# Sixteen-wide inverse blocks, with their join issued in the running chain, in a kernel that interleaves RWKV-7 and sparse attention

## The chip, the cores and the metric

The kernel runs on one core of a Trainium2 chip. The metric is the device time of one execution in microseconds (us), as the median of three runs. TensorE, VectorE (DVE in the rows), ScalarE (ACT), GpSimd (POOL) and SyncE (SP, which issues most loads and stores) each work through a queue of their own in a fixed order.

## The reference

One step of a layer on 1,056 tokens: 1,024 of a prompt and 32 of a running stream (the "sample"). The normalised input is projected once; half of the columns feed sparse attention (8 query heads, 4 key heads, each query keeps its top k keys by a lightweight index), the other half feed RWKV-7 time mixing (8 heads of 64). Both results are joined, projected, and followed by an MLP with 4,096 hidden units. What matters here is RWKV's recurrence over tokens, per head with a 64 x 64 state:

```python
def step(S, inp):
    r_t, w_t, k_t, v_t, kk_t, b_t = inp
    s_kk = jnp.einsum('bhvk,bhk->bhv', S, kk_t)
    S = S * w_t[:, :, None, :] - s_kk[..., None] * b_t[:, :, None, :] + v_t[..., None] * k_t[:, :, None, :]
    return S, jnp.einsum('bhvk,bhk->bhv', S, r_t)
s_fin, y = lax.scan(step, wkv0, ...)
```

The kernel computes it by chunks of 64 tokens. Within a chunk the dependence of a token on the ones before is a triangular 64 x 64 system per head, and the chunk needs the inverse of that matrix.

## The kernel before

A first phase projects the input and finds the top k keys (`topk`, and the masks made of it). The last phase is the output projection and the MLP. Between them, from about 450 to 930 us of the profile, two generators are advanced in turn, one step each: `attn_all` (36 items: 4 key heads times 9 token tiles, each with scores, softmax, transposes and products) and `rwkv_all`. The program is written in that interleaved order; a scheduler then fixes the order of every engine's queue from the program order, the dependences and ranks, with its own estimate of durations. `tc.high_priority(n)` moves instructions n places ahead in rank, a negative n behind. All of `rwkv_all` stands under OFF (-200), a unit's chain additionally under BOFF (+300) and a unit's preparation under FOFF (-100).

RWKV works on five units: units 0 to 3 are 256 prompt tokens each, in four chunks, and unit 4 is the sample in one chunk. Round i of `rwkv_all` runs three generators side by side:

- `rwkv_front` of unit i+2 loads the unit's rows, makes the decays and keys, and for each chunk the matrix G of all eight heads (matmuls of line 712, mask on VectorE in line 715). The G buffer is the one of unit i, so chunk c waits until unit i has done its chunk c. At the end `lane_inverse` inverts the 32 x 32 diagonal blocks.
- `rwkv_back` of unit i is the chain: it first calls `rwkv_join`, which makes 64 x 64 inverses out of the 32 x 32 blocks with two rounds of 32 small TensorE calls (lines 768 and 776; every such call stands as two instructions in the trace). Then, chunk by chunk, pR, copy to `rh` (line 882), pU, copies to VU, pS, new state `st`, pY, copy to `y` on ScalarE (line 911). All four accumulators take the same single PSUM buffer `pc`.
- `rwkv_norm` of unit i-1 normalises and gates the result and stores it.

`lane_inverse` lays a unit's 32 x 32 blocks out with one pair of heads and chunks per partition: four VectorE transposes with every input column taken twice (line 824, 32 x 1,024 each), then 31 steps of two element-wise instructions on GpSimd (lines 829 and 831) on up to 136 elements per partition, and four transposes back into G (line 835), and for the full units two more into `X1` (line 840). The start value is loaded by DMA from `half`.

After both generators, `project_early` multiplies the first three token tiles by the output weights (line 1256), whose split into high and low parts waits until unit 3 is done.

Of the kernel before, what the change touches and what calls it, by code (L numbers as in the profile page):

```python
# [32 lines left out]
def pack(I):  # L33
    A={n:np.ascontiguousarray(I[n]) for n in RAW}
    A['pvec']=pvec(I)
    A['norms']=np.ascontiguousarray(np.concatenate([I['norm_mix'],I['norm_ffn']]))
    A['gains']=np.ascontiguousarray(np.stack([I['q_gain'][0],I['k_gain'][0],I['kidx_ln_g'][0],I['kidx_ln_b'][0]]))
    A['rope']=rope(); A['ident']=np.eye(128,dtype=np.float32); A['gmask']=gmask()
    p=np.arange(128)
    A['bones']=(p[:,None]//64==np.arange(2)[None]).astype(np.float32)  # L40
    A['bone2']=(p[:,None]//64==p[None]//64).astype(np.float32)
    s,m=np.arange(32)[None,:,None],np.arange(16)[None,None]
    A['half']=(s==2*m+(p[:,None,None]%32)//16).astype(np.float32).reshape(128,512)
    return A


# [7 lines left out]
F32 = mybir.dt.float32  # L54
# [509 lines left out]
def rwkv_setup(S):  # L564
    nc, I = S.nc, S.I
    S.gm = S.rs.tile([128, 128], F32, name="gm")
    nc.sync.dma_start(S.gm, I["gmask"])
    S.bones = S.rs.tile([128, 2], F32, name="bones")
    nc.sync.dma_start(S.bones, I["bones"])
    bone2 = S.rs.tile([128, 128], F32, name="tmp", bufs=2)  # L570
    nc.sync.dma_start(bone2, I["bone2"])
    S.cen = S.rs.tile([128, 128], F32, name="cen")
    nc.vector.scalar_tensor_tensor(S.cen, bone2, -1.0 / 64, S.ident, op0=ALU.mult, op1=ALU.add)
    S.ones = S.rs.tile([128, 64], F32, name="ones")
    nc.gpsimd.memset(S.ones, 1.0)
    S.hv = S.rs.tile([128, 4, 4], F32, name="hv")
    nc.gpsimd.tensor_scalar(S.hv[:, 0], S.pv[:, 56:60], 0.5, None, op0=ALU.mult)
    nc.gpsimd.tensor_scalar(S.hv[:, 1], S.pv[:, 56:60], -0.5, 1.0, op0=ALU.mult, op1=ALU.add)
    nc.gpsimd.tensor_scalar(S.hv[:, 2:4].rearrange("p a b -> p (a b)"), S.pv[:, 44:52], 0.5, None, op0=ALU.mult)
    S.g2 = S.rs.tile([96, 512], F32, name="g2")  # L580
    nc.sync.dma_start(S.g2, I["g2"][0])

    w = S.rs.tile([32, 2, 512], F32, name="tmp", bufs=2)
    nc.sync.dma_start(w[:, 0], I["w2"][0])
    nc.sync.dma_start(w[:, 1], I["a2"][0])
    S.w3 = S.rs.tile([96, 2, 512], F32R, name="w3")
# [9 lines left out]
def rwkv_front(S, u, U, B):  # L596
# [3 lines left out]
    w = n // NC  # L600
# [116 lines left out]

    while B and B.done < B.NC:
        yield
    lane_inverse(S, U, nc.vector if u in DINV else nc.gpsimd)  # L720
    S.fronts += 1
    yield

# [33 lines left out]
def rwkv_join(S, ps, U):  # L757

    nc = S.nc
    X1 = U.X1.rearrange("p (c h) t -> p c h t", c=4)  # L760

    def pc():
        return ps.tile([128, 512], F32, name="pc", bufs=1).rearrange("p (a b c) -> p a b c", a=4, b=4)
    p = pc()
    for cc in range(4):
        for hp in range(4):
            for par, b in ((0, 64), (1, 0)):
                nc.tensor.matmul(p[b + 32:b + 64, cc, hp], U.G[b:b + 32, par, cc, hp, 32:64], X1[b:b + 32, cc, hp],
                                 start=True, stop=True)
    for par, b in ((0, 64), (1, 0)):  # L770
        nc.scalar.copy(X1[b + 32:b + 64], p[b + 32:b + 64])
    p = pc()
    for cc in range(4):
        for hp in range(4):
            for par, b in ((0, 64), (1, 0)):
# [34 lines left out]
def lane_inverse(S, U, eng):  # L810


    nc = S.nc
    L = S.rf2.tile([128, 32, 32], F32, name="L", bufs=1)
    Y = S.rf2.tile([128, 32, 32], F32, name="Yl", bufs=1)[:, :, 0:16]
    tm = S.rf2.tile([128, 144], F32, name="tl", bufs=1)
    G = U.G
    nc.sync.dma_start(Y, S.I["half"].rearrange("p (s m) -> p s m", s=32))

    def part(par, p, b):  # L820
        return G[p:p + 32, par, :, :, 32 * b:32 * b + 32].rearrange("p c h t -> p (c h) t")
    groups = [(0, 64, 0), (0, 96, 1), (1, 0, 0), (1, 32, 1)]
    for g in groups:
        nc.vector.transpose(L[g[1]:g[1] + 32].rearrange("p s t -> p t s"),  # L824
                            part(*g).rearrange("p l t -> p t l")[:, :, None, :].to_broadcast([32, 32, 2, 16]))
    for j in range(31, 0, -1):
        m, w = j // 2, 16 - j // 2
        t_ = tm[:, 0:j * w].rearrange("p (a b) -> p a b", a=j)
        eng.tensor_tensor(t_, L[:, 0:j, j:j + 1].to_broadcast([128, j, w]),  # L829
                          Y[:, j:j + 1, m:16].to_broadcast([128, j, w]), op=ALU.mult)  # L830
        eng.tensor_tensor(Y[:, 0:j, m:16], Y[:, 0:j, m:16], t_, op=ALU.add)  # L831

    for g in groups:
        if g[2] == 0 or U.w == 64:
            nc.vector.transpose(part(*g).rearrange("p l (m d) -> p m d l", d=2), Y[g[1]:g[1] + 32].rearrange("p s m -> p m s"))
    if U.w == 64:
        U.X1 = S.P[0].tile([128, 16, 32], F32, name="X1", bufs=1)
        for par, p, b in groups:
            if b == 0:
                nc.vector.transpose(U.X1[p:p + 32], part(par, p, b))  # L840


def rwkv_back(S, rp, ps, U, state):
# [8 lines left out]
    def quarter(p):  # L852
        return p[:, 0:256].rearrange("p (a b) -> p a b", a=4)
    for c in range(len(U.tok), min(NC, 2)):
        U.tok.append(rwkv_tokens(S, rp, ps, U, c))
    tok = U.tok
    if w == 64:
        rwkv_join(S, ps, U)
    yield
    st = state.get("st")  # L860
    if u == 4:
# [7 lines left out]
    for c in range(NC):  # L869
# [31 lines left out]
            nc.vector.tensor_tensor(sn, pS, st, op=ALU.add)  # L901
            nc.vector.tensor_tensor(sn, sn, pcb, op=ALU.mult)
        yield
        pY = quarter(pc())
        for hp, par in pairs:
            nc.tensor.matmul(pY[PAR[par], hp], VU[:, par, hp], G[:, par, c, hp, 64:128], start=(hp == 0), stop=(first and hp == 3))
        if not first:
# [3 lines left out]
        nc.scalar.copy(y[:, :, c], pY)  # L911
        st = sn
        U.done = c + 1
        if c + 2 < NC:
            tok.append(rwkv_tokens(S, rp, ps, U, c + 2))
        elif U.next and TOKN and len(U.next.tok) < U.next.NC:
            U.next.tok.append(rwkv_tokens(S, rp, ps, U.next, len(U.next.tok)))
# [54 lines left out]


YB = 2


def rwkv_all(S, order):
# [23 lines left out]
    def norm(i):  # L1001
        if i >= 0:
            yield from rwkv_norm(S, S.P[0], S.ps, units[i])
        if 0 <= i + 2 < len(order):
            rwkv_prelude(S, S.P[0], units[i + 2])
    for i in range(-2, len(order) + 1):
        gens = []
        B = front = None
# [2 lines left out]
            gens.append(back := rwkv_back(S, S.P[0], S.ps, B, state))  # L1011
        if i >= -1:
            gens.append(norm(i - 1))
            if i == 0:
                shift_rows(S, S.P[0], S.ps)
        if i + 2 < len(order):
# [361 lines left out]
ATT0 = 0  # L1378
BOFF = 300
TOKB = 3  # L1380
FOFF = -100
EARLY = 0
POOLU0 = ('k','tha','KB0')
POOLU = ('tha',)
# [20 lines left out]
CKT = 6  # L1405
LAGT = 3
KNB = 5
OFF = -200


def body(tc, I, O, dbg=None):
# [126 lines left out]
```

## Time and profile before

| | us |
|---|---|
| median of 3 runs (lowest, highest) | 1,794.74 (1,794.37, 1,796.54) |
| the profiled execution | 1,798.12 |
| its span, first to last instruction | 1,796.3 |
| TensorE busy in the span | 1,663.9 (93%) |
| mean granted TensorE clock | 0.927 of full speed |

The busy time of an engine is the union of its instructions' times. The granted clock is 1 at 2.4 GHz and 0.5 at 1.2 GHz; a value in between is the mean over a stretch that holds both.

### The profile page before, as it was taken

The page shows a single profiled execution, that of the slowest core. Times are in us where ns is not written, and L with a number is a line of the kernel's source. Part 1 is how long each engine was busy: PE and PEld are TensorE (multiplying, and loading weights), DVE is VectorE, ACT ScalarE, POOL GpSimd, SP SyncE. Part 2 cuts the span into 40 slices and gives each one's busy share as a digit, 9 for nine tenths or more (in the row PEclk, how much of TensorE's full clock was granted, in tenths as well). Part 3 has the DMA queues.
Part 4 walks back from the last instruction along what each step waited for, and adds up shares of the span by engine and source line. Part 5 has one row for each costly group of instructions (what it writes and reads, how often), then busy time and mean ns, then how long its engine had stood idle before and what let it go on. Part 6 is the DMA issues. An engine that isn't in the chain of part 4 may idle for free.

```text
span 1796.3 us, 30013 instructions
## 1 busy us (share of the span) xinstructions
PE 1663.9 (93%) x11686; PEld 1509.2 (84%) x11686; DVE 936.1 (52%) x1996; ACT 707.6 (39%) x1549; POOL 618.6 (34%) x919
## 2 busy tenths in 40 slices
PE   7999979986569898999899999999999999999999
PEld 6787779986456777767678799999999999999998
DVE  6477889975878687577562533222222222222224
ACT  6365667897446344344641331222222121212120
POOL 7468863353543443056210021222222222222120
PEclk9999989996559697798899999999999999999999
DMA  7211131323110202140323341111111111111105
GB/s 218 54 36 43 42 88 64 110 68 92 29 27 14 40 24 57 26 101 17 98 76 123 121 125 49 46 48 45 49 37 53 42 53 42 47 44 51 36 16 172
DMA packets 180775, 113.25 MB, mean 63 GB/s; under 512 B 51969, under 2 KB 169817, under 8 KB 180633
## 3 DMA queue, kind: packets, MB, share of 16 engines
q1 hardware_dynamic: 171800, 107.00, 21.4%
q10 hardware_dynamic: 8832, 4.33, 0.9%
q8 instruction: 92, 1.51, 0.4%
q14 instruction: 51, 0.41, 0.1%
HBM read 86.29 MB, written 25.01 MB: 62 GB/s over the span
## 4 chain that ended last, share of the span: by engine, by line
PE 63%; DVE 12%; ACT 5%; POOL 4%; issue 3%; DMA 2%; SPq 0%; DVEq 0%; ACTq 0%; POOLq 0%
PE pd L1320 20%; PE pr L1340 10%; PE pc L1340 5%; PE po L1340 5%; PE pd L1256 3%; PE po L1139 2%; DVE AR L342 2%; ACT AR L362 2%; PE ptr L1123 2%; PE pr L1256 2%; PE acc L440 2%; DVE L L824 1%; PE pr L712 1%; POOL tl L829 1%; POOL Yl L831 1%
## 5 line engine op out<-in xcount | busy, mean ns | idle before, releaser
L1320 PE MATMUL pd<-hh,w1h 128*128 128x352 f32 x768 | 248.6, 324 | 2.2 <-issue 1.4
L1320 PE MATMUL pd<-hh,w1l 128*128 128x352 f32 x768 | 248.2, 323 | 0.7 <-DVE w1l L1187 0.7
L1320 PE MATMUL pd<-hl,w1h 128*128 128x352 f32 x768 | 247.5, 322 | 0.0
L1326 DVE TENSOR_TENSOR h2l<-rl,h2h 128x352 fp32r<-128x352 f32 x96 | 56.9, 592 | 277.3 <-ACT h2h L1325 277.3
L1324 POOL TENSOR_TENSOR rl<-rl 128x352 f32<-128x352 f32 x96 | 85.2, 888 | 215.5 <-ACT rl L1323 215.5
L1186 ACT CAST w2h<-w2r 128x512 fp32r<-128x512 f32 x64 | 39.7, 621 | 293.0 <-PE po L1340 144.8
L1320 PEld LDWEIGHTS pd<-hh,w1h 128*128 128x128 f32 x768 | 144.7, 188 | 2.8 <-issue 1.7
L1320 PEld LDWEIGHTS pd<-hh,w1l 128*128 128x128 f32 x768 | 144.8, 189 | 0.9 <-DVE w1l L1187 0.9
L1320 PEld LDWEIGHTS pd<-hl,w1h 128*128 128x128 f32 x768 | 145.3, 189 | 0.0
L1187 POOL TENSOR_TENSOR w2l<-w2r,w2h 128x512 fp32r<-128x512 f32 x32 | 41.6, 1299 | 299.3 <-ACT w2h L1186 288.8
L1340 PE MATMUL pr<-h2h,w2l 128*128 128x352 f32 x384 | 124.3, 324 | 0.0
L1340 PE MATMUL pr<-h2h,w2h 128*128 128x352 f32 x384 | 124.3, 324 | 0.0
L1340 PE MATMUL pr<-h2l,w2h 128*128 128x352 f32 x384 | 124.1, 323 | 0.0
L362 ACT ACTIVATE AR<-G,cnd 128x768 bf16<-128x768 f32 (+2 forms) x93 | 96.7, 1040 | 42.2 <-DVE cnd L367 36.8
L1323 ACT ACTIVATE rl<-pd 128x352 f32<-128x352 f32 x96 | 44.3, 463 | 143.4 <-PE pd L1320 136.9
L1346 DVE TENSOR_TENSOR ya<-ya,pr 128x352 f32<-128x352 f32 x84 | 43.8, 521 | 101.0 <-PE pr L1340 101.0
L829 POOL TENSOR_TENSOR tl<-L,Yl 128x56 f32<-128x56 f32 (+22 forms) x155 | 65.9, 425 | 60.5 <-DVE L L824 50.0
L1105 ACT ACTIVATE s<-s,m 32x544 f32<-32x544 f32 (+8 forms) x72 | 55.4, 770 | 74.8 <-DVE m L1102 74.6
L1123 PE MATMUL ptr<-ident,s 128*128 128x128 f32 (+2 forms) x328 | 69.4, 321 | 16.2 <-ACT s L1105 11.2
L1325 ACT CAST h2h<-rl 128x352 fp32r<-128x352 f32 x96 | 46.6, 485 | 75.3 <-POOL rl L1324 75.3
L1340 PEld LDWEIGHTS pr<-h2l,w2h 128*128 128x128 f32 x384 | 72.3, 188 | 0.1
L1340 PEld LDWEIGHTS pr<-h2h,w2h 128*128 128x128 f32 x384 | 72.2, 188 | 0.1
(443 smaller groups left out, 4655.1 us busy)
## 6 DMA issues: line engine op xcount, KB each, us to landing
w1r<-in_w_ff_dram SPq DMA_DIRECT2D x32, 512.0 KB, 4.1
w2r<-in_w_ff_dram SPq DMA_DIRECT2D x64, 256.0 KB, 2.9
zsd<-zm SPq DMA_DIRECT2D x12, 528.0 KB, 2.7
wraw<-in_w_in_dram SPq DMA_DIRECT2D x24, 256.0 KB, 2.7
wraw<-in_w_in_dram SPq DMA_DIRECT2D x40, 128.0 KB, 2.2
x<-in_x_prompt_dram SPq DMA_DIRECT2D x8, 512.0 KB, 5.0
hres<-hd ACTq DMA_DIRECT2D x16, 256.0 KB, 3.3
out_dram<-hres SPq DMA_DIRECT2D x16, 256.0 KB, 2.3
```

Source lines behind the costliest of these rows:

```text
L362: nc.scalar.activation(junk2[:r, :n], S.sc[t][:r, :n], AF.Sign, bias=c_of(j, r), scale=-1.0, accum_out=cnt[:r, j:j + 1])
L829: eng.tensor_tensor(t_, L[:, 0:j, j:j + 1].to_broadcast([128, j, w]), Y[:, j:j + 1, m:16].to_broadcast([128, j, w]), op=ALU.mult)
L1105: nc.scalar.activation(s, s, AF.Exp, bias=m[:, i:i + 1], scale=-1.0, accum_out=w.m[:, 6 + h:7 + h])
L1123: nc.tensor.transpose(p[:x, i, h, :r], w.s[h][:, c0 + i * 128:c0 + i * 128 + x], S.ident[:r, :r])
L1256: nc.tensor.matmul(acc[:r], a[:, k], b, start=(i == 0), stop=(i == 23))
L1320: nc.tensor.matmul(acc, a[:, k], m[:, k, o:o + n], start=(i == 0), stop=(i == 23))
L1323: nc.scalar.activation(rl, acc, AF.Relu)
L1324: nc.gpsimd.tensor_tensor(rl, rl, rl, op=ALU.mult)
L1325: nc.scalar.copy(h2h[:, o:o + n], rl)
L1326: nc.vector.tensor_tensor(h2l[:, o:o + n], rl, h2h[:, o:o + n].bitcast(F32), op=ALU.subtract)
L1340: nc.tensor.matmul(acc, a[:, k], m[:, o:o + n], start=(i == 0), stop=(i == 11))
L1346: nc.vector.tensor_tensor(y, y, acc, op=ALU.add)
```

## The change

`lane_inverse` now inverts 16 x 16 blocks: the transposes take every column once (32 x 512), one VectorE instruction adds the two halves of each lane together under a mask, GpSimd runs 15 steps of two instructions on up to 64 elements, ScalarE makes two masked copies, and two 128-partition transposes give `Dg` and `Et`. It returns a function `finish`, which makes the 32 x 32 inverses on TensorE: two stages of 64 calls of 32 x 32, with a mask between them and four additions into G behind them. `finish` of unit i+1 is called in the chain of unit i after chunk 1 (line `U.next.finish()`), `rwkv_join` after chunk 2; for unit 0 a new generator `first` issues the tokens of two chunks, waits JOIN0 rounds, and calls both. The two PSUM tiles of `rwkv_join`, and pY, move from `pc` to the two buffers of `pr`. OFF goes from -200 to 0 and FOFF from -100 to 0. The constant `half` is replaced by `eye16` and `lanes`.

```diff
-    lane_inverse(S, U, nc.vector if u in DINV else nc.gpsimd)
+    U.finish = lane_inverse(S, U, nc.vector if u in DINV else nc.gpsimd)
...
     def pc():      # in rwkv_join
-        return ps.tile([128, 512], F32, name="pc", bufs=1)...
+        return ps.tile([128, 512], F32, name="pr", bufs=PRB)...
...
     for g in groups:
         nc.vector.transpose(L[g[1]:g[1] + 32].rearrange("p s t -> p t s"),
-                            part(*g).rearrange("p l t -> p t l")[:, :, None, :].to_broadcast([32, 32, 2, 16]))
-    for j in range(31, 0, -1):
-        m, w = j // 2, 16 - j // 2
+                            part(*g).rearrange("p l (d t) -> p t d l", d=2))
+    nc.vector.scalar_tensor_tensor(Lc, L[:, 0:16], S.lm[:, 0:1], L[:, 16:32], op0=ALU.mult, op1=ALU.add)
+    for j in range(15, 0, -1):
+        w = 16 - j
         t_ = tm[:, 0:j * w].rearrange("p (a b) -> p a b", a=j)
-        eng.tensor_tensor(t_, L[:, 0:j, j:j + 1]..., Y[:, j:j + 1, m:16]..., op=ALU.mult)
-        eng.tensor_tensor(Y[:, 0:j, m:16], Y[:, 0:j, m:16], t_, op=ALU.add)
-    for g in groups:
-        if g[2] == 0 or U.w == 64:
-            nc.vector.transpose(part(*g).rearrange("p l (m d) -> p m d l", d=2), Y[g[1]:g[1] + 32].rearrange("p s m -> p m s"))
+        eng.tensor_tensor(t_, Lc[:, 0:j, j:j + 1]..., Y[:, j:j + 1, j:16]..., op=ALU.mult)
+        eng.tensor_tensor(Y[:, 0:j, j:16], Y[:, 0:j, j:16], t_, op=ALU.add)
+    for i in range(2):
+        nc.scalar.activation(Y2[:, 16 * i:16 * i + 16], Y, AF.Copy, scale=S.lm[:, i:i + 1])
+    nc.vector.transpose(Dg.rearrange("p l (d m) -> p m d l", d=2), Y2.rearrange("p s m -> p m s"))
+    nc.vector.transpose(Et, Dg)
+    def finish():
+        def pj():
+            return S.ps.tile([128, 16, 32], F32, name=S.pr[0], bufs=S.pr[1])
+        p = pj()
+        for l in range(16):
+            for g in groups:
+                q = slice(g[1], g[1] + 32)
+                nc.tensor.matmul(p[q, l], part(*g)[:, l], Et[q, l], start=True, stop=True)
+        nc.vector.tensor_tensor(Z, p, S.lm[:, None, 2:34].to_broadcast([128, 16, 32]), op=ALU.mult)
+        p = pj()
+        for l in range(16):
+            for g in groups:
+                q = slice(g[1], g[1] + 32)
+                nc.tensor.matmul(p[q, l], Z[q, l], Dg[q, l], start=True, stop=True)
+        for g in groups:
+            if g[2] == 0 or U.w == 64:
+                q = slice(g[1], g[1] + 32)
+                nc.vector.tensor_tensor(part(*g), p[q], Dg[q], op=ALU.add)
+        if U.w == 64:
+            ...  # X1, as before
+    return finish
...
-    if w == 64:            # at the head of rwkv_back
-        rwkv_join(S, ps, U)
...
-        pY = quarter(pc())
+        pY = quarter(ps.tile([128, 512], F32, name="pr", bufs=PRB))
...
         U.done = c + 1
+        if U.next and c == min(1, NC - 1):
+            U.next.finish()
+        if U.next and c == 2 and U.next.w == 64:
+            rwkv_join(S, ps, U.next)
...
+    def first():           # a generator beside the front of unit 1
+        U = units[0]
+        for c in range(2):
+            U.tok.append(rwkv_tokens(S, S.P[0], S.ps, U, c))
+            yield
+        for _ in range(JOIN0):
+            yield
+        U.finish()
+        for _ in range(2):
+            yield
+        rwkv_join(S, S.ps, U)
+        yield
...
+JOIN0 = 4
-FOFF = -100
+FOFF = 0
-OFF = -200
+OFF = 0
```

## Rows read from the trace of the kernel before

**Rows 1.** The page's slices: the span in 40 equal parts, in tenths.
```profile
PE   7999979986569898999899999999999999999999
PEclk9999989996559697798899999999999999999999
```

**Rows 2.** Windows: stretch, its length, then PE, PEld, DVE, ACT, POOL busy, PEclk, DMA, GB/s.
```profile
454.00:518.00 64.00, 29.85 (x141) 20.88 (x139) 55.86 (x103) 25.56 (x61) 39.30 (x69) 0.53 0.13 26
518.00:569.00 51.00, 46.80 (x400) 37.01 (x402) 35.03 (x80) 25.91 (x55) 6.06 (x13) 0.76 0.10 22
569.00:642.00 73.00, 66.25 (x679) 53.19 (x680) 50.53 (x119) 32.86 (x90) 34.55 (x69) 0.74 0.18 32
642.00:656.00 14.00, 10.18 (x214) 8.28 (x214) 13.05 (x14) 5.20 (x10) 2.52 (x10) 0.83 0.19 50
656.00:731.00 75.00, 69.28 (x709) 54.86 (x709) 53.61 (x130) 34.26 (x86) 32.99 (x67) 0.85 0.18 41
731.00:752.00 21.00, 21.00 (x261) 16.81 (x257) 8.68 (x17) 7.44 (x21) 1.03 (x3) 0.63 0.14 31
752.00:830.00 78.00, 71.27 (x704) 53.53 (x702) 61.33 (x133) 32.16 (x81) 39.24 (x100) 0.86 0.25 63
830.00:842.00 12.00, 12.00 (x218) 10.04 (x214) 4.51 (x13) 6.45 (x14) 7.66 (x13) 0.88 0.04 12
842.00:889.00 47.00, 43.31 (x600) 33.58 (x597) 28.92 (x84) 28.19 (x76) 14.27 (x35) 0.96 0.32 95
889.00:933.00 44.00, 40.39 (x382) 31.16 (x382) 31.73 (x87) 23.19 (x53) 13.66 (x12) 0.92 0.19 49
```

**Rows 3.** Groups by line, 454 to 933 us: busy us, mean ns, idle before.
```profile
L824 DVE STREAM_TRANSPOSE L<-G 32x1024 f32<-32x1024 f32 x20 | 41.0, 2050 | 0.3
L835 DVE STREAM_TRANSPOSE G<-Yl 32x512 f32<-32x512 f32 x18 | 20.3, 1130 | 7.6 <-POOL Yl L831 7.2
L715 DVE TENSOR_TENSOR G<-pr,gm 128x512 f32<-128x512 f32 x28 | 19.1, 689 | 10.4 <-PE pr L712 10.0
L911 ACT COPY y<-pc 128x256 f32<-128x256 f32 x17 | 6.2, 365 | 17.2 <-PE pc L910 14.9 <-PE pc L906 2.3
```

**Rows 4.** Timeline of POOL, inverse of units 0 and 2: start, duration.
```profile
464.41 0.25 POOL L829 TENSOR_TENSOR tl<-L,Yl 128x31 f32<-128x31 f32 x1 [6.85 <-DVE L L824]
...
509.73 0.22 POOL L831 TENSOR_TENSOR Yl<-Yl,tl 128x16 f32<-128x16 f32 x1
...
654.78 0.28 POOL L829 TENSOR_TENSOR tl<-L,Yl 128x58 f32<-128x58 f32 x1
655.14 0.31 POOL L831 TENSOR_TENSOR Yl<-Yl,tl 128x58 f32<-128x58 f32 x1
655.53 0.28 POOL L829 TENSOR_TENSOR tl<-L,Yl 128x56 f32<-128x56 f32 x1
```

**Rows 5.** Timeline of PE: a stage of the join at either clock.
```profile
529.42 1.92 PE L776 MATMUL pc<-G,X 32*32 32x32 f32 x64
...
832.24 1.20 PE L768 MATMUL pc<-X,G 32*32 32x32 f32 x64
```

**Rows 6.** Windows around these two stages.
```profile
527.00:533.00 6.00, 6.00 (x83) 5.60 (x82) 0.76 (x2) 1.89 (x5) 0.00 (x0) 0.50 0.05 14
831.00:834.00 3.00, 3.00 (x81) 2.45 (x80) 1.05 (x3) 2.12 (x5) 2.27 (x6) 1.00 0.02 5
```

**Rows 7.** Timeline of PE: attention's last product and the output projection's first matmul.
```profile
930.61 0.33 PE L1143 MATMUL po<-ident,x 128*128 128x128 f32 x1
...
933.03 0.49 PE L1256 MATMUL pr<-G 128*128 128x512 f32 x1
```

**Rows 8.** Timeline of DVE: the copy `rh` of chunks in units 0 and 3.
```profile
569.61 0.42 DVE L882 COPY rh<-pc 128x256 f32<-128x256 f32 x1 [0.64 <-PE pc L876]
...
589.98 0.42 DVE L882 COPY rh<-pc 128x256 f32<-128x256 f32 x1
...
842.88 0.42 DVE L882 COPY rh<-pc 128x256 f32<-128x256 f32 x1 [2.06 <-PE pc L880]
...
876.38 0.42 DVE L882 COPY rh<-pc 128x256 f32<-128x256 f32 x1
```

More of the change, by code (lines that the diff above doesn't have):

```diff
@@ L41, in pack @@
     A['bone2']=(p[:,None]//64==p[None]//64).astype(np.float32)
-    s,m=np.arange(32)[None,:,None],np.arange(16)[None,None]
-    A['half']=(s==2*m+(p[:,None,None]%32)//16).astype(np.float32).reshape(128,512)
+    A['eye16']=np.tile(np.eye(16,dtype=np.float32).reshape(1,256),(128,1))
+    h=(p[:,None]%32)//16
+    A['lanes']=np.concatenate([h==0,h==1,(h==1)&(np.arange(32)[None]<16)],1).astype(np.float32)
     return A
@@ L573, in rwkv_setup @@
     nc.vector.scalar_tensor_tensor(S.cen, bone2, -1.0 / 64, S.ident, op0=ALU.mult, op1=ALU.add)
+    S.lm = S.rs.tile([128, 34], F32, name="lm")
+    nc.sync.dma_start(S.lm, I["lanes"])
     S.ones = S.rs.tile([128, 64], F32, name="ones")
@@ L762, in pc @@
     def pc():
-        return ps.tile([128, 512], F32, name="pc", bufs=1).rearrange("p (a b c) -> p a b c", a=4, b=4)
+        return ps.tile([128, 512], F32, name="pr", bufs=PRB).rearrange("p (a b c) -> p a b c", a=4, b=4)
     p = pc()
@@ L813, in lane_inverse, with v @@
     nc = S.nc
-    L = S.rf2.tile([128, 32, 32], F32, name="L", bufs=1)
-    Y = S.rf2.tile([128, 32, 32], F32, name="Yl", bufs=1)[:, :, 0:16]
-    tm = S.rf2.tile([128, 144], F32, name="tl", bufs=1)
+    t0 = S.rf2.tile([128, 1024], F32, name="L", bufs=1)
+    t1 = S.rf2.tile([128, 1024], F32, name="Yl", bufs=1)
+    tm = S.rf2.tile([128, 64], F32, name="tl", bufs=1)
     G = U.G
-    nc.sync.dma_start(Y, S.I["half"].rearrange("p (s m) -> p s m", s=32))
+    def v(t, o, m, w):
+        return t[:, o:o + m * w].rearrange("p (a b) -> p a b", a=m)
+    L, Y2 = v(t0, 0, 32, 16), v(t0, 512, 32, 16)
+    Y, Lc, Dg = v(t1, 0, 16, 16), v(t1, 256, 16, 16), v(t1, 512, 16, 32)
+    Et, Z = v(t0, 0, 16, 32), v(t0, 512, 16, 32)
+    nc.sync.dma_start(t1[:, 0:256], S.I["eye16"])
     def part(par, p, b):
@@ L824, in lane_inverse @@
         nc.vector.transpose(L[g[1]:g[1] + 32].rearrange("p s t -> p t s"),
-                            part(*g).rearrange("p l t -> p t l")[:, :, None, :].to_broadcast([32, 32, 2, 16]))
-    for j in range(31, 0, -1):
-        m, w = j // 2, 16 - j // 2
+                            part(*g).rearrange("p l (d t) -> p t d l", d=2))
+    nc.vector.scalar_tensor_tensor(Lc, L[:, 0:16], S.lm[:, 0:1], L[:, 16:32], op0=ALU.mult, op1=ALU.add)
+    for j in range(15, 0, -1):
+        w = 16 - j
         t_ = tm[:, 0:j * w].rearrange("p (a b) -> p a b", a=j)
-        eng.tensor_tensor(t_, L[:, 0:j, j:j + 1].to_broadcast([128, j, w]),
-                          Y[:, j:j + 1, m:16].to_broadcast([128, j, w]), op=ALU.mult)
-        eng.tensor_tensor(Y[:, 0:j, m:16], Y[:, 0:j, m:16], t_, op=ALU.add)
@@ L833, in lane_inverse @@
-    for g in groups:
-        if g[2] == 0 or U.w == 64:
-            nc.vector.transpose(part(*g).rearrange("p l (m d) -> p m d l", d=2), Y[g[1]:g[1] + 32].rearrange("p s m -> p m s"))
[L836 to L840, printed above, removed]
+        eng.tensor_tensor(t_, Lc[:, 0:j, j:j + 1].to_broadcast([128, j, w]),
+                          Y[:, j:j + 1, j:16].to_broadcast([128, j, w]), op=ALU.mult)
@@ new lines, in lane_inverse @@
+        eng.tensor_tensor(Y[:, 0:j, j:16], Y[:, 0:j, j:16], t_, op=ALU.add)
[22 more added lines that the diff above has]
+        if U.w == 64:
+            U.X1 = S.P[0].tile([128, 16, 32], F32, name="X1", bufs=1)
+            for par, p, b in groups:
+                if b == 0:
+                    nc.vector.transpose(U.X1[p:p + 32], part(par, p, b))
@@ L1013, in rwkv_all @@
             gens.append(norm(i - 1))
+            if i == -1:
+                gens.append(first())
             if i == 0:
```

## The prediction

> **What bounds the kernel now.** I began with the page's slices [rows 1]. From about 1,080 us on TensorE is busy without a break at the full clock: that is the MLP, which the change does not touch. The slices between roughly 400 and 930 us are different: TensorE is at 5 to 9 tenths and its granted clock at 5 to 9 tenths too. That is where attention and RWKV run side by side, so I looked only there. From the timelines of VectorE and ScalarE I took the times at which a unit's chain starts (first copy `rh`) and ends (copy `y` of its fourth chunk) and cut the stretch 454 to 933 us at them [rows 2]: the first unit's inverse (454 to 518), its join and waiting (518 to 569), the chains of units 0 to 3 (569 to 642, 656 to 731, 752 to 830, 842 to 889), the gaps between them (14, 21 and 12 us), and the sample unit with its norm (889 to 933).
>
> The reader should see three things there. First, TensorE is busy 410.3 of 479 us (the sum of the rows' PE column), but the rows' clock, weighted with their length, is 0.79, so some 42% of the time is at 1.2 GHz (weighted with TensorE's busy time 0.81: 38%, 157 us). Idle are 68.7 us; 34.2 of them stand in the first stretch alone, where VectorE is busy 55.86 of 64 us. Second, the gaps between the chains are gaps of the chain, not of TensorE: it is busy 10.18 of 14, 21 of 21 and 12 of 12 us in them, with other work. Third, POOL is nowhere near full after the first stretch. So the bound is mostly TensorE, in order and partly at half clock, and only in the first stretch the way through POOL and VectorE. The two threads end together: attention's last product at 930.61, RWKV's last norm just before 933.03, when the output projection starts [rows 7]. Both must get shorter, or share better, for the end to move.
>
> **The inverse.** Before, 31 steps of two POOL instructions; for unit 0 the first starts at 464.41 and the last at 509.73, 45.5 us [rows 4]. After, 15 steps on at most 64 elements per partition. Instructions with 56 to 58 elements follow each other by 0.36 to 0.39 us [rows 4], so 30 of them take about 11 us undisturbed. POOL was disturbed in the first stretch (39.3 us busy for 45.5 us of inverse and what lies between [rows 2]), so I take 16: 29 us sooner. The four input transposes halve from 1,024 to 512 elements: they cost 2.05 us each before, a 512-element one 1.13 [rows 3], so about 3.7 us less. The four output transposes (4.5 us) go; in their place VectorE gets one multiply-add of 256 elements, two transposes of 512 on all partitions, and in `finish` one masked copy and four additions out of PSUM, 0.69 us each by the mask row [rows 3]: together some 0.5 + 2 x 1.1 + 5 x 0.69 = 6.2 us. VectorE's net is 4.5 + 3.7 - 6.2 = 2 us less per unit. ScalarE gets two copies of 256 elements, 0.37 us each by the copy of `y` [rows 3]; the small DMAs (`eye16`, half the bytes of `half`, and `lanes` once) go through SP's queue well ahead of use. None of these is on the path after unit 0, because the inverse of the later units runs under the chain of the unit before: what hides it is that chain, 47 to 78 us long [rows 2]; without that cover it would cost its whole length.
>
> In the first stretch the join of unit 0 can therefore come about 30 us earlier. TensorE idles 34.2 us there, but VectorE has only 8.1 us free, as it ends the top-k masks and feeds attention. Nothing gained if VectorE keeps the stretch as long as it is, at most 30 us if TensorE's work fills the hole: I take **-12 us**, nearer to VectorE's free time.
>
> **The join of 16 into 32 (`finish`).** Two stages of 64 calls per unit, five units. The existing join has 32 calls per stage, which stand as 64 instructions and take 1.92 us at the half clock and 1.20 at the full one [rows 5, 6]. A stage of `finish` is twice that: 2.4 to 3.84 us; ten stages cost 24 to 38 us. At the region's mix (42% at half) that is 30. The new calls go round four diagonal positions where the join goes round two. No row shows four; if four go in the time of the join's two, a stage costs what the join's does, 15 in all, and below there is only one instruction's 1.92/64 = 0.03 us per stage, next to nothing. I take **+22 us**, the middle between 15 and 30, and keep 0 and 38 for the range.
>
> The Trainium skill, page TensorE: Matmul & The Clock Gate, Part 3 (Packing small matmuls), says that small matmuls in different row groups of the array run at the same time, so that four positions cost hardly more than one. By that rule the term would be at most 15 and the forecast 7 us lower, 1,774, still inside its own case; no row here shows four positions, and what the join's rows show of two [rows 5] does not contradict it.
>
> **Where join and finish are issued.** The join moves from the head of the next unit's chain into the running one after chunk 2, `finish` goes after chunk 1; both take buffers of `pr`, and so does pY, so that the one `pc` buffer is free sooner for the next chunk's pR. Per chunk this takes pY, its two groups of matmuls and ScalarE's copy (0.37 us) out of the chain. The gaps of 14 + 21 + 12 us and the 38 us from the join's second stage (529.42 + 1.92 = 531.3) to the first chunk's copy at 569.61 [rows 5, 8] can close, as `first()` issues unit 0's tokens early. What that is worth is TensorE's idle time from 518 to 889, 30.9 us [rows 2], and the clock. Below nothing is possible (the same work moves), above all 31. I take a third, **-10 us**; and for the 21 us at 0.63, where some 15 us are at half clock and 1.92/1.20 = 1.6 is the ratio of the two clocks, 15.5 x (1 - 1/1.6) = **-6 us**.
>
> **Ranks.** OFF from -200 to 0 and FOFF from -100 to 0 put RWKV's instructions earlier in every queue against attention's, on TensorE, VectorE, ScalarE, POOL and the loads on SP. They add no work. If RWKV ends well before 933, attention's last items run alone and the early projection, which follows both and now keeps TensorE full from 933 on, can fill their holes, as the weights' split needs only unit 3's end. TensorE idles 3.6 us in the last stretch now; attention alone would leave more. From 0 to -15, I take **-8 us**. The order that the ranks give in between I take at 0, with 20 us to either side.
>
> Sum: -12 + 22 - 10 - 6 - 8 = **-14 us**. The profiled execution took 1,798.1 us for its span of 1,796.3; so 1,784.1, and the median of the runs lies 3.4 lower: **1,781 us**.
>
> **Rivals.** *A, both threads pack.* TensorE's idle share falls to that of 842 to 889 (3.7 of 47, 8%): 38 instead of 69 us idle, -31. Half of the 157 us at the low clock go to the high one: -78 x (1 - 1/1.6) = -29. `finish` costs its 24. Together -36: 1,759. For it: that stretch holds RWKV's chain and attention at 0.96 of the clock, and a chunk every 11 us against 20 in unit 0 [rows 2, 8]. Against: no front runs there.
> *B, TensorE is the bound and small matmuls keep it at 1.2 GHz (slower).* `finish` costs its 38, the first stretch stays as long as VectorE makes it, the gaps close without gain since TensorE was busy in them, the tail gives 8 and some 5 of idle time: +25, 1,820. It decides once `finish` costs over 36 us or the idle time stays. For it: 0.63 in the 21 us gap at 100% busy, whose work is of just that kind [rows 2].
> *C, the threads only trade.* RWKV ends sooner, attention as much later: `finish` is paid out of the first stretch and the tail, 0: 1,795. For it: both end within 3 us of each other now.
> *D, TensorE waits in order for `finish`.* A unit's inverse can start only when the unit two before has ended, and takes 4.5 + 0.5 + 16 + 3 + queues, about 27 us; `finish` stands two chunks into the next chain. At 20 us a chunk there is room (40), at 11 there are 22 and TensorE stands for 5 to 6 us in each of three units, with attention behind it: 18 us, 1,799. It decides below 14 us a chunk.
>
> **Chances and range.** Forecast 0.42, A 0.18, C 0.14, B 0.16, D 0.10. A change under 0.2%, 3.6 us, can hardly be told from none. Faster: 0.40 of the forecast's and all of A, 0.58. Same: C's 0.12 and 0.02 of the forecast's, 0.14. Slower: B, D and 0.02 of C, 0.28. The range leaves out the far half of A and of B: 1,750 to 1,815; the forecast's own, with the bounds of `finish` and of the first stretch, is 1,765 to 1,794.
>
> **What would show it.** Right: POOL's inverse of unit 0 under 20 us; the first `rh` near 530 instead of 570; no gap between the chains; stages of `finish` of 2 to 4 us; the early projection's start before 925. Wrong: TensorE waiting in front of `finish`'s lines; a first stretch as long as now; a chunk still at 20 us; a lower clock from 500 to 800 us; or attention alone for long at the end with TensorE idle.

## The result, and the profile after

The changed kernel takes **1,804.22 us** in the median of 5 runs (1,801.38 to 1,811.06), the kernel before 1,794.74 beside it; the ratio is **1.0058, interval 1.0034 to 1.0083**: slower by some 10 us, where I had forecast 14 faster. The profiled execution took 1,804.16 us for a span of 1,802.4.

The page's slices, TensorE's busy share and its granted clock, beside [rows 1]:

```profile
PE   7999979986688998999989999999999999999999
...
PEclk9999989996686797996989999999999999999999
```

The clock is a little better than before in the region (0.85 against 0.83 in the last rows of the next two fences), and TensorE is at least as busy: neither a lower clock nor an idle TensorE explains the loss. The windows of the kernel after, cut at its own stages (unit 0's inverse; to the end of its wait for the join; units 0 and 1; ...; the last up to RWKV's last matmul; then the whole region to the output projection's last matmul):

```profile
454.00:518.00 64.00, 40.42 (x239) 30.57 (x238) 56.05 (x138) 33.74 (x85) 18.77 (x41) 0.64 0.13 35
518.00:576.00 58.00, 49.61 (x703) 36.73 (x702) 40.44 (x83) 26.37 (x54) 14.10 (x38) 0.82 0.05 14
576.00:642.00 66.00, 64.39 (x989) 52.77 (x988) 39.04 (x107) 27.81 (x76) 5.97 (x10) 0.80 0.12 33
642.00:746.00 104.00, 98.42 (x1282) 78.72 (x1281) 69.01 (x170) 48.90 (x125) 21.36 (x47) 0.85 0.15 42
746.00:833.00 87.00, 81.25 (x1099) 62.75 (x1099) 56.39 (x138) 35.04 (x85) 23.97 (x73) 0.85 0.18 57
833.00:897.00 64.00, 60.77 (x946) 47.40 (x945) 34.79 (x99) 33.83 (x89) 7.69 (x10) 0.93 0.23 68
897.00:943.00 46.00, 37.74 (x325) 28.87 (x322) 28.30 (x72) 20.09 (x43) 12.64 (x10) 0.85 0.30 82
454.00:1043.60 589.60, 532.93 (x6034) 417.61 (x6033) 363.21 (x863) 248.52 (x596) 111.19 (x237) 0.85 0.19 57
```

and the same region of the kernel before:

```profile
454.00:1037.60 583.60, 514.38 (x4758) 402.34 (x4757) 386.60 (x841) 246.28 (x589) 198.00 (x397) 0.83 0.22 58
```

The last rows of the two fences hold the whole difference. The region got 589.6 - 583.6 = 6.0 us longer, and the spans differ by 1,802.4 - 1,796.3 = 6.1: everything happens here. TensorE's busy time grew by 532.9 - 514.4 = 18.5 us, and its idle time shrank from 69.2 to 56.7, by 12.5. Of these, 10.6 are in the first stretch (64 - 29.85 = 34.15 idle before [rows 2], 64 - 40.42 = 23.58 now). Everywhere else only 2 us of idle time went. POOL's work halved (198 to 111 us) and bought nothing by itself.

Lines of the changed kernel below: 856 and 862 are the two stages of `finish`, 906 and 910 are pR, 918 is pU, 920 ScalarE's copy to VU, 936 and 940 pY, 941 the copy to `y`, 1002 the norm, 1195 attention's last transpose of an item, 1308 the output projection. Where TensorE's new time is, by groups between 454 and 944 us (columns: calls | busy us, mean ns of one | idle before):

```profile
L856 PE MATMUL pr<-L,G 32*32 32x32 f32 x640 | 15.9, 209 | 0.0
L862 PE MATMUL pr<-Yl,L 32*32 32x32 f32 x640 | 7.5, 194 | 0.5 <-issue 0.4
```

The first and the second stage of `finish` have the same number of the same instructions, and the first costs twice the second. TensorE's timeline shows why: the first row is unit 0's first stage, the last is half of an undisturbed pR, and those between are from unit 2's first stage.

```profile
526.75 1.29 PE L856 MATMUL pr<-L,G 32*32 32x32 f32 x128
...
686.26 0.24 PE L856 MATMUL pr<-L,G 32*32 32x32 f32 x2
686.44 0.33 PE L906 MATMUL pc<-VU,G 64*64 64x64 f32 x2
686.69 0.24 PE L856 MATMUL pr<-L,G 32*32 32x32 f32 x2
686.86 0.33 PE L906 MATMUL pc<-VU,G 64*64 64x64 f32 x2
687.12 0.24 PE L856 MATMUL pr<-L,G 32*32 32x32 f32 x2
...
693.35 1.17 PE L856 MATMUL pr<-L,G 32*32 32x32 f32 x68
694.45 1.12 PE L918 MATMUL pc<-rh,G 64*64 64x64 f32 x16
695.50 0.64 PE L856 MATMUL pr<-L,G 32*32 32x32 f32 x30
...
706.21 0.68 PE L906 MATMUL pc<-VU,G 64*64 64x64 f32 x16
```

Undisturbed, 128 instructions take 1.29 us, 10 ns each. In unit 2 the scheduler dealt 15 of the stage's 64 calls out one by one with the calls of the chain's next pR (lines 906 and 910, 64 x 64), and a pair of calls comes every 0.43 us (686.26, 686.69, 687.12). The other 49 stand in two blocks around pU. That stage lasts from 686.3 to 696.1, and unit 3's, mixed in the same way, from 786.0 to 795.6. Unit 1's first stage, from 583.6 to 588.2, is only cut into three pieces. Apart, at the full clock, stage, pR and pU would take 1.29 + 1.15 + 0.68 = 3.1 us of these 9.8 (pR of another chunk runs from 632.93 to 634.08, its pU takes 0.68). The granted clock falls to its lower level, 1.2 GHz, within this piece while TensorE is busy throughout, as two windows show (granted clock is the third figure from the end); in unit 3's mixed stage it is 0.72 between 786 and 796, after 1.00 in the 8 us before:

```profile
686.00:688.50 2.50, 2.50 (x36) 1.89 (x32) 0.76 (x2) 0.37 (x1) 0.00 (x0) 1.00 0.00 0
690.00:696.00 6.00, 6.00 (x140) 4.85 (x139) 0.81 (x2) 0.00 (x0) 0.00 (x0) 0.61 0.01 3
```

Unit 0's stage stands at 526.75, although its inverse left POOL at 479.6 (the first row below; 509.95 before [rows 4]), VectorE's transpose into `Dg` ran at 481.54 and the one into `Et`, the last input, ended at 483.9: 43 us in TensorE's queue, behind attention and unit 1's preparation. ScalarE's first copy to VU is at 564.23, against 574.1 before.

```profile
479.28 0.32 POOL L842 TENSOR_TENSOR Yl<-Yl,tl 128x15 f32<-128x15 f32 x1
...
481.54 1.06 DVE L845 STREAM_TRANSPOSE Yl<-L 128x512 f32<-128x512 f32 x1
```

At the end, attention's last transpose comes 7 us earlier than in [rows 7], and RWKV's last matmul 10 us later. The output projection's first matmuls (935.94) now stand between those of RWKV's last norm, 3 us later than before:

```profile
924.00 0.33 PE L1195 MATMUL po<-ident,x 128*128 128x128 f32 x1
...
935.94 0.80 PE L1308 MATMUL pd<-G,o 128*128 128x512 f32 x1 [1.50 <-ACT o L1294]
...
942.52 0.53 PE L1002 MATMUL pr<-zg,g 96*128 96x32 f32 x4
...
943.44 0.40 PE L1308 MATMUL pr<-G 128*128 128x512 f32 x1
```

### The profile page after: what moved, and what is told of

It reads as the page before. It is cut to its first block, busy times and chain, and to the rows that moved or that the text cites. A ratio compares the mean times of both kernels' runs of the same rounds, so it can differ in the third digit from the quotient of the medians.

```text
span 1802.4 us, 32468 instructions
## 1 busy us (share of the span) xinstructions
PE 1683.8 (93%) x12966; PEld 1525.7 (85%) x12966; DVE 915.8 (51%) x2016; ACT 711.5 (39%) x1559; POOL 530.5 (29%) x759
## 3 DMA queue, kind: packets, MB, share of 16 engines
q1 hardware_dynamic: 152104, 106.37, 20.2%
## 4 chain that ended last, share of the span: by engine, by line
PE 51%; DMA 1%; ACT 1%; DVE 1%; issue 0%; SPq 0%; POOL 0%; DVEq 0%; ACTq 0%
PE pd L1372 20%; PE pr L1392 10%; PE pc L1392 5%; PE po L1392 5%; PE pd L1308 3%; PE pr L1308 2%; PE po L1191 1%; PE ptr L1175 0%; PE ptr L1406 0%; DMA of<-od 0%; PE ptr L145 0%; PE pc L925 0%; DMA w1r<-in_w_ff_dram 0%; PE pr L749 0%; ACT G L1274 0%
## 5 line engine op out<-in xcount | busy, mean ns | idle before, releaser
L1392 PEld LDWEIGHTS pr<-h2h,w2l 128*128 128x128 f32 x384 | 72.3, 188 | 0.1
```

The costliest lines, as they stand in the source:

```text
L1392: nc.tensor.matmul(acc, a[:, k], m[:, o:o + n], start=(i == 0), stop=(i == 11))
```

## The experiments

Each was timed beside the kernel before, in 4 to 12 executions; "after" is the changed kernel, with ratio 1.0058. Differences between two versions are those of their ratios, times 1,796. A profiled execution need not be near the median: those of e1, e7 and e17 were the longest of each (1,807.2, 1,791.5, 1,846.8), that of e6 by far the shortest (1,801.8), and those of e14 and e15 among the shortest (1,774.7, 1,771.1). So the ends of these traces are not compared with medians. My theories: **M**, the call-by-call mixing of 32 x 32 with 64 x 64 calls costs the 10 us; **F**, the first unit's `finish` is issued 43 us late; **P**, pY waits for a buffer of `pr` behind the norm and the front; and as rival **R**, the new ranks cost the time.

**e1, finish ahead in rank** (after; in TensorE's queue no stage alternates call by call any more: each stands in one to three pieces).
```diff
-            U.next.finish()
+            with S.tc.high_priority(1000):
+                U.next.finish()
```


> The changed kernel with finish of the next unit ranked 1,000 places ahead, so that its 64 calls per stage stand together in TensorE's queue. M (mixing: in units 1 to 3 the first stage of finish, 32x32, alternates call by call with the chain's pR, 64x64, at 0.43 us a pair against about 0.09 apart, some 14 us in all) expects the stage to take 1.3 to 2.5 us in every unit in place of 4.6, 9.8 and 9.6, and 1,790 us (1,784 to 1,796). P (the chain waits in the queue for the two pr buffers, where pY now stands behind fronts and norms) expects no change, 1,804, give or take 3. R (the raised ranks of RWKV cost the time) expects 1,804 or more.

Measured: 1,793.36 us, 0.9998 (0.9978 to 1.0018): the loss is gone. The groups of this kernel:

```profile
L862 PE MATMUL pr<-Yl,L 32*32 32x32 f32 x640 | 7.9, 200 | 2.5 <-issue 2.5
L856 PE MATMUL pr<-L,G 32*32 32x32 f32 x640 | 6.6, 193 | 1.5 <-issue 1.5
```

14.5 us instead of 23.4.

**e2, pY back to pc** (after).
```diff
-        pY = quarter(ps.tile([128, 512], F32, name="pr", bufs=PRB))
+        pY = quarter(pc())
```


> The changed kernel with pY back in the single buffer pc; finish and the join stay in pr. P expects the copy of y to follow its VU copy within 10 us in place of up to 42, the chains to shorten and 1,790 us or less. M expects that only unit 3's first stage of finish is still mixed with pR in the queue (units 1 and 2 are not), so 6 to 8 us less, 1,797, and no gain beyond that. R expects no change, 1,804.

Measured: 1,802.48, 1.0043 (1.0020 to 1.0066). Not to be told from after; unit 3's stage is still mixed (775.7 to 786.9 us), while unit 2's now takes 2.9 us. M had expected 6 to 8 us from that; 3 came, and the intervals leave both 0 and 8 open.

**e3, the old ranks** (after with FOFF -100, OFF -200).

> The changed kernel with OFF = -200 and FOFF = -100 as before. R expects the loss to go, 1,795 or less. M expects no gain, 1,802 to 1,808, as two units' first stages of finish are still mixed with pR. P expects no gain or a loss, 1,804 to 1,812, as RWKV's work waits longer behind attention.

Measured: 1,823.06, 1.0148 (1.0132 to 1.0165). R falls: the new ranks are worth 16 us (0.0090) to this kernel. M's 1,802 to 1,808 missed too. With the old ranks more is mixed than M had counted: unit 0's two stages last 7.8 and 10.3 us, beside 11.8 and 10.3 for the first stages of units 2 and 3, so part of the 16 us may be mixing.

**e4, the new ranks on the kernel before** (FOFF and OFF to 0, nothing else).

> The kernel before with OFF = 0 and FOFF = 0 alone. R expects it slower by the same 9 us or more, 1,804. M and P expect no part of the loss here: 1,795 give or take 4, or a gain of some us if the ranks by themselves help.

Measured: 1,797.13, 0.9994 (0.9974 to 1.0013). Alone they change nothing that can be told from noise.

**e5, finish called behind the tokens of chunk c+2** (after, ranks as they are): M against "any higher rank helps".
```diff
-        if U.next and c == min(1, NC - 1):
-            U.next.finish()
...
         elif U.next and TOKN and len(U.next.tok) < U.next.NC:
             U.next.tok.append(...)
+        if U.next and c == min(1, NC - 1):
+            U.next.finish()
```


> The changed kernel, ranks untouched, with the call of finish moved behind the tokens of chunk c + 2, a few instructions later in the program; in TensorE's queue the first stage of finish then stands in one or two pieces in every unit and the second in three to five. M (alternating 32x32 and 64x64 calls costs the 10 us) expects what the rank did: 1,793, give or take 4, and first stages of 1.3 to 2.5 us. K (it was the rank, by which finish and so the next chain come earlier) expects no gain: 1,804.

Measured: 1,796.94, 1.0004 (0.9988 to 1.0020). Its first stages stand in one or two pieces and last 1.3 to 2.4 us, by program order alone, and it gains what e1 does. The mean granted clock of its executions is that of after's, 0.932, so the gain is not the clock's.

**e6, a rank of 100 instead of 1000**, which mixes the second stage instead of the first.

> The changed kernel with finish ranked 100 places ahead in place of 1,000. Now the first stage stands together, but the second alternates with pY and pR in four units (13 to 21 pieces). M expects the loss to be back or larger, 1,804 to 1,812, with second stages of 5 to 10 us in four units. K expects the same as with 1,000: 1,793.

Measured: 1,824.07, 1.0134 (1.0096 to 1.0171). The second stages now last 8 to 14 us in four units (586.2 to 600.6, 694.1 to 703.5, 789.1 to 797.3, 861.3 to 871.8), and the kernel is 14 us worse than after. One of its six executions, the profiled one, took only 1,801.8; the other five took 1,816.4 to 1,828.3. With e1 and e5, M is shown from both sides: two different edits that take the alternation away gain the 10 us, and one that moves it to the second stage brings the loss back.

**e7, e1 and the first unit at once.**
```diff
-JOIN0 = 4
+JOIN0 = 0
...
-        U.finish()
-        for _ in range(2):
-            yield
-        rwkv_join(S, S.ps, U)
+        with S.tc.high_priority(1000):
+            U.finish()
+            rwkv_join(S, S.ps, U)
```


> The kernel of the first experiment (finish 1,000 ahead), and for unit 0 no waiting rounds (JOIN0 = 0) and finish and join 1,000 ahead too. If the first unit's start is on the path (F), its chain begins some 35 us earlier, near 528 in place of 564 at the first VU copy, and the time falls by 10 us or more, to 1,783 or less. If TensorE's and VectorE's total work sets the end (W), the chain starts earlier but the end stays: 1,793, give or take 4.

Measured: **1,776.66, 0.9879 (0.9865 to 0.9894)**, the lowest median of this study. Its five executions go from 1,771.8 to 1,791.5, and their plain mean is 0.991 of the kernel before's, outside that interval; so differences from e7 are also given by plain means below. Its timeline:

```profile
484.90 1.75 PE L856 MATMUL pr<-L,G 32*32 32x32 f32 x128
489.31 1.80 PE L862 MATMUL pr<-Yl,L 32*32 32x32 f32 x128 [1.85 <-DVE L L857]
...
516.11 0.36 ACT L920 COPY VU<-pc 64x256 f32<-64x256 f32 x1
```

Stage 1 stands 42 us earlier than in after and the first copy to VU 48 us earlier.

**e8, e1 and pY in pc.**

> The kernel of the first experiment with pY back in pc. P (pY waiting for pr behind fronts and norms holds up tokens and chain) expects a gain on top of the unmixed finish: 1,786 or less. Without P: 1,793, give or take 4; slower if the single pc buffer holds up the next chunk's pR.

Measured: 1,789.45, 0.9958 (0.9940 to 0.9977), 7 us under e1.

**e9, e7 and pY in pc.**

> The changed kernel with both remedies: every finish ahead in rank with the first unit's finish and join at once, and pY back in pc. If the costs of the first unit's late finish and of pY in pr lie in different places, they add: ratio 0.988 - 0.004 = 0.984, about 1,768 us. If the chain of the later units only gives pY's 7 us to attention, which ends the stretch then, it stays at 0.988, about 1,775.

Measured: 1,787.50, 0.9951 (0.9936 to 0.9967): neither; 13 us (0.0072) worse than e7 by the ratios, 9 by plain means. RWKV's last matmul is at 908 us here and attention's at 942; in e7 they are at 925 and 923.

**e10, e9 with each finish matmul issued twice in a row.**
```diff
-                nc.tensor.matmul(p[q, l], part(*g)[:, l], Et[q, l], start=True, stop=True)
+                for _ in range(2):
+                    nc.tensor.matmul(p[q, l], part(*g)[:, l], Et[q, l], start=True, stop=True)
```
(and the same for the second stage.)

> The same kernel with each of the two matmul groups of finish issued twice. Ten more packed stages of 1.29 us at the full clock and some 2 at the half one are 13 to 20 us of TensorE. If TensorE's work sets the end of the stretch (the forecast's finish term as the price of the stages), the time is 13 to 20 us over the single version, ratio about 0.995; if the packed stages lie in TensorE's idle time, less than 5 us over it.

Measured: 1,826.97, 1.0149 (1.0126 to 1.0172): 36 us over e9 by the ratios, twice what either reading allowed. I put it down to two calls in a row at one position, which would no longer overlap, and so e17 repeats the calls in turn. The rows do not bear that out:

```profile
L864 PE MATMUL pr<-Yl,L 32*32 32x32 f32 x1280 | 16.5, 210 | 15.0 <-issue 7.9 <-DVE L L858 7.0
L857 PE MATMUL pr<-L,G 32*32 32x32 f32 x1280 | 15.1, 200 | 8.5 <-issue 8.5
```

The instructions take 31.6 us, about twice e9's 14.7, so they still overlap; but TensorE also stopped for 16.4 us in the middle of the stages with nothing that the profile shows to wait for ("issue").

**e11, e9 with finish and join at the head of the unit's own chain**, as the kernel before had its join.
```diff
+    if U.i:      # head of rwkv_back
+        with S.tc.high_priority(1000):
+            U.finish()
+        if w == 64:
+            rwkv_join(S, ps, U)
...          # and the two calls behind chunks 1 and 2 removed
```


> The same kernel as the first of these with finish and join of units 1 to 3 (finish alone for the sample) at the head of their own chain, as the kernel before had its join, instead of in the running one. If issuing them in the running chain closes the gaps between the chains, as the forecast has it (10 us and 6 of clock), this is 10 to 16 us slower than the first: ratio about 0.993. If the gaps stay whichever way it is issued, within 4 us of it.

Measured: 1,792.50, 0.9974 (0.9957 to 0.9992): 4 us over e9, with the two intervals together 0 to 8. Yet the gaps between the chains, from a unit's last copy to VU to the next unit's first, are 44, 43, 35 and 34 us here and 34, 20, 14 and 29 in e9: 156 against 97.

**e12, the kernel before with the join's tiles and pY in pr; e13, pY alone; e14, the join's tiles alone.**
```diff
-        return ps.tile([128, 512], F32, name="pc", bufs=1)...   # rwkv_join: e12, e14
+        return ps.tile([128, 512], F32, name="pr", bufs=PRB)...
-        pY = quarter(pc())                                      # e12, e13
+        pY = quarter(ps.tile([128, 512], F32, name="pr", bufs=PRB))
```


> The kernel before, with the join's two PSUM tiles and pY in the two pr buffers and nothing else changed. If pY's wait behind the norm's and the front's tiles costs by itself, 5 to 8 us slower, ratio 1.003 to 1.0045. If it only costs beside the new ranks and the finish stages, which also take pr, no change; if freeing pc gives what the forecast has for it, up to 10 us faster, 0.9945.

> The kernel before with pY alone in the two pr buffers (the join stays in pc). The kernel with both moved ran 42 us over before; in its trace the first unit's join comes 38 us later and three copies of y come 27 to 28 us after their chunk's VU. If pY carries the loss: 25 to 40 us slower, ratio 1.014 to 1.022. If the join carries it: under 5 us slower, below 1.003.

> The kernel before with the join's two tiles alone in pr (pY stays in pc). If the join's wait behind the front's tiles in the first stretch carries the loss: 25 to 40 us slower, ratio 1.014 to 1.022, and the first join again near 567 us instead of 528. If pY carries it: under 5 us slower, below 1.003.

Measured: e12 1,839.46, 1.0226 (1.0204 to 1.0248); e13 1,824.37, **1.0152 (1.0128 to 1.0176)**; e14 1,786.93, 0.9940 (0.9914 to 0.9966). pY alone costs 27 us, the join's tiles alone gain 11. But both together cost 42, far over e12's three expectations and 26 more than the sum of the two; no run says where these come from. Unit 1's first chunk in e13, ScalarE's copies and then TensorE:

```profile
654.83 0.37 ACT L890 COPY VU<-pc 64x256 f32<-64x256 f32 x1 [1.50 <-DVE VU L889]
...
699.88 0.37 ACT L911 COPY y<-pr 128x256 f32<-128x256 f32 x1 [0.57 <-PE pr L910]
```

```profile
694.15 1.10 PE L968 MATMUL pr<-zg,g 96*128 96x256 f32 x4 [2.65 <-DVE y L961]
...
695.41 1.03 PE L968 MATMUL pr<-zg,g 96*128 96x256 f32 x4
...
698.59 0.63 PE L906 MATMUL pr<-G,VU 128*64 128x64 f32 x16
699.15 0.68 PE L910 MATMUL pr<-AR,st 64*64 64x64 f32 x16
```

pY (in this kernel's numbering lines 906 and 910) comes 44 us after its VU: the `pr` buffers go first to the preparation of unit 3 and the norm of unit 0, whose last matmuls (line 968) waited for VectorE and stand just ahead. In the kernel before the copy to `y` was at 667.1, 5.6 us after VU at 661.5. After has the same wait: VU at 639.05, `y` at 681.12.

**e15, e9 with OFF -50; e16, after with the first unit at once and no other edit.**

> The kernel with the first unit at once, finish ahead and pY in pc, with OFF -50 instead of 0. That kernel ran 1,787 us, 11 over its twin with pY in pr, and in its trace RWKV ends at 908 and attention at 942, against 925 and 923 in the twin's. If it lost because RWKV ran too far ahead of attention, a rank of -50 brings both ends near 925 and the time to the twin's or below it: 1,770 to 1,777, ratio 0.985 to 0.989. If TensorE's total work decides whatever thread ends last, no change: 0.995.

> The changed kernel with one edit, the first unit's finish and join at once; the finish of the later units keeps its rank, and its first stage stays mixed call by call with pR in units 2, 3 and the sample. Mixing cost 10 us and the first unit's late finish 17 to 20 by the earlier runs: if these are separate terms, 1,785 to 1,788, ratio 0.994 to 0.996. If an early first unit is worth nothing as long as the mixing holds TensorE: 1.005 as the changed kernel.

Measured: e15 1,780.03, 0.9923 (0.9897 to 0.9949), between the two expectations; but attention still ends 34 us behind RWKV (929 and 895), so the rank did not bring the two ends together, as its theory has it, and the gain over e9 has another cause. e16 1,795.34, 0.9999 (0.9983 to 1.0015): 11 us under after, so F costs without M's remedy too.

**e17, e9 with a full round over the four positions, twice.**
```diff
-        for l in range(16):
+        for l in list(range(16)) * 2:
```
(in both stages)

> As e10, each of finish's two matmul groups twice, but a whole round over the four positions and then the same round again, so that two calls of one position never follow each other. In e10 they did, and its ten stages took 47.8 us instead of 16.6 in the single version: 31 more, for 39 us of time. Here a stage should be 2.6 us at the full clock, 14 to 17 us more in all. If each us of TensorE in this stretch costs one of the time: 14 to 21 us over the single version's 1,787, ratio 1.003 to 1.007. If e10's loss was its longer chain and not TensorE's time: under 6 us over it, below 0.999.

Measured: 1,831.05, 1.0189 (1.0166 to 1.0212): 43 us over e9. TensorE's groups and a piece of its timeline:

```profile
L862 PE MATMUL pr<-Yl,L 32*32 32x32 f32 x1280 | 14.7, 205 | 16.5 <-issue 10.5 <-DVE L L857 6.1
L856 PE MATMUL pr<-L,G 32*32 32x32 f32 x1280 | 14.0, 202 | 8.9 <-issue 8.9
```

```profile
575.24 1.99 PE L856 MATMUL pr<-L,G 32*32 32x32 f32 x212
579.24 0.58 PE L856 MATMUL pr<-L,G 32*32 32x32 f32 x44 [2.01 <-issue]
```

The instructions cost what was expected, 28.7 us instead of e9's 14.7. But here, too, the stages stop, for about 2 us each: 19.4 us of "issue". And the rest of TensorE's work runs slower, with the region's granted clock at 0.79 in the profile (0.86 in e9). So 14 us of TensorE's time cannot be priced by this run, nor by e10; what both show is that the added instructions and stops, some 32 us each time, were not hidden in TensorE's idle time.

**e18, e7 with OFF -50.**

> The version with the first unit at once and finish ahead, pY left in pr, with OFF -50 instead of 0. With pY in pc this rank gained 5 to 7 us (0.9951 to 0.9923) and left attention 34 us behind RWKV. If the rank helps by what it does in the first stretch (VectorE 3 us less busy there, the first chain ahead), here too: about 1,771, ratio 0.983 to 0.987. If pY's wait in pr grows with a lower rank of the norm and the front, as in the kernel before at -200: slower than 1,777, 0.990 to 0.996.

Measured: 1,789.34, 0.9957 (0.9941 to 0.9974), 14 us over e7 by the ratios, 9 by plain means. The wait of pY is no longer than in e7 (unit 1: VU 620.6, `y` 664.9, against 627.4 and 675.6), so the theory whose number came out is not confirmed by its mechanism.

## Why the prediction was wrong, step by step

Three steps failed. `finish` was priced as blocks that run undisturbed, and its mixing with pR costs 11 us (e1). The first unit's join was to come 30 us earlier, and its `finish` waited 43 us in TensorE's queue, which costs 11 (e16). And issuing in the running chain was to earn 16 us, where e11 finds 4. With the first two remedied (e7) the median is 1,777, near the forecast's 1,781, but since the third term is not earned, that is in part luck.

**The sum by TensorE.** The forecast's sum holds +22 for `finish` and -6 of clock, so +16 of busy time, and -12, -10 and -8 of idle time. Measured: +18.5 busy, -12.5 idle. The busy side came out near, but by luck, as the mixing's 9 us stand in it; the idle side failed.

**First stretch, -12.** TensorE's idle time there fell by 10.6 us, as the term said, but not in the way it said. The hole was filled by attention and preparation, not by unit 0's join. POOL's steps took 20.2 us (459.4 to 479.6; 16 forecast, 45.5 before), and then `finish` waited 43 us, behind other work in TensorE's queue, since the `first` generator issues it JOIN0 rounds late. My "first `rh` near 530" looked only at when the data is ready. With the call at once, the chain does start at 516, and the kernel gains: 11 us (e16 against after), 21 (e7 against e1; 16 by plain means).

**`finish`, +22.** The size is right, 23.4 measured, but by luck: the working is wrong. Four positions do pack: 1.29 us a stage at the full clock, under my 2.4, and all ten take 14.5 us unmixed (e1), the 15 of the case that I had set beside the 30. This is what I had quoted from the Trainium skill, page TensorE: Matmul & The Clock Gate, Part 3 (Packing small matmuls); the trace agrees, with 128 instructions at four positions in 1.29 us where 64 at the join's two take 1.20 [rows 5]. The other 9 us, and the time that the mixed pR's take with them, are the mixing, which I had not priced: I priced a stage as a block and took "issued in the running chain" for a place in the queue. That place means that the scheduler may deal the stage out between another thread's calls of another tile size. The Trainium skill, page TensorEngine Tiling (Array Packing), section Key Properties, says that changing the tiling mode drains TensorE; it gives no price, and the trace fits it with 0.43 us for a pair of calls at the full clock. That the drain is the reason is not shown: no run alternates calls of one size in this way. The mixing was none of my rivals. It is the loss: e1 and e5 are 0.9998 and 1.0004.

**Issuing in the running chain and freeing pc, -10 and -6.** This is the term that failed outright. Outside the first stretch only 2 of 35 us of idle time went. The gaps do close when the join is issued early and nothing else stands in the way (97 against 156 us, e9 and e11), but that is worth about 4 us of time (0 to 8), where 16 were booked: the reader was told in [rows 2] that TensorE is busy in the gaps, and I booked a gain there all the same. In after itself the gaps stayed at 31, 28, 29 and 27 us, 114 together, against 119 before. And "taking pY out of the chain" put it behind two other users of `pr`: on the kernel before, 27 us slower (e13). In after the copy to `y` comes up to 42 us after VU, but what that costs there is not settled (e2: 3 us, within noise). The 1.6 in the clock's term is the ratio of one stage's times at the two clocks; the clocks themselves stand as 2 to 1, which would have made the term -8.

**Ranks, -8, and 0 for the order.** The tail did not come: RWKV ends last, at 943, and TensorE idles 8.3 us in the last 46 (3.6 of 44 before [rows 2]). The ranks with their order, which I took at -8 and at 0 with 20 to either side, are together worth -16 us to this kernel (e3, where the mixing differs too) and nothing to the old one (e4).

**The rivals.** D expected TensorE to stand in front of `finish`, and 1,799. The time is near, the mechanism is not: line 856 has no idle time before it. B, TensorE the bound, is nearest: "the idle time stays" came true outside the first stretch, and added work was not hidden in e10 and e17; but its price of 38 us for `finish` is far over the 23.4 measured. A is what e7 shows in part: the idle time falls by 23 us (69.2 to 46.5 in e7's profile). The forecast's own range of 1,765 to 1,794 does not follow from the bounds that it names: 0 and 38 for `finish` and 0 to -30 for the first stretch give 1,741 to 1,809.

**What stays open.** M is worth 11 us alone (e1), F 11 alone (e16), both 32 (e7; 27 by plain means); I can't say where the other 5 to 10 come from. Nor why pY in pc gains 7 us over e1, loses 13 against e7 and gains 6 against e18: at the new ranks its sign was not settled, and none of my theories predicts e7's lead over its neighbours, whose size rests on five executions.

## What to carry to other kernels

When a thread's small matmuls are issued inside another thread, look at the queue that results, not only at the place of the call: a group of small calls that alternates with calls of another tile size can cost several times what the two take apart, so keep it in one piece, by rank or by program order. Data that is ready early gains little while its consumer stands late in its engine's queue. And before a step is moved to another buffer, look who holds that buffer and what these wait for.

## What the runs showed of the hardware

- Calls of 32 x 32 and 64 x 64 in turn: 0.43 us for each pair of calls at the full clock (0.64 at the half one, e6 from 697.96 to 700.52), where the same two plus two instructions apart take 0.02 (2 x 1.29/128) and 0.09 (2 x 0.68/16).
- Eight of e17's ten packed stages of 256 instructions stop for about 2 us with no wait in the profile, as after the 212 instructions above (575.24 + 1.99 to 579.24). So do eight of e10's. A packet of the instruction queue (16 KB each by the profile's page, 1.84 MB in 112) stands in the trace at 576.8, just ahead of that pause. That TensorE outran its supply of instructions is a guess from this, not shown.
- The mean granted clock differs between executions of one kernel, and the time goes with it: e14's twelve runs go from 1,772 us at 0.942 to 1,795 at 0.923, e15's from 1,771 at 0.944 to 1,795 at 0.926. In e14's profile (0.939) TensorE's busy time in the region is 492.5 us for the same instructions that took 514.4 before, and its idle time is the same, 68.5 against 69.2: so in that execution, one of e14's fastest, the gain is the clock.
